# The end of a causal convolution: another split of the last channel block's taps, and a rearranged normalization ahead of the next product

## The chip, the cores and the metric

The kernel runs on one core of one Trainium2 chip. A core has a matrix engine (TensorE, PE in the profile), a vector engine (VectorE, DVE), a scalar engine (ScalarE, ACT) and GpSimd (POOL), each with its own queue of instructions that it works off in order; SP issues the weight loads. Engines wait for each other by semaphores. TensorE reads SBUF and writes PSUM, which has banks of 512 fp32 columns on 128 partitions. The metric is the device time of one execution in microseconds (us); lower is better.

## The reference, cut to what matters

The model is a trunk of two layers for 256 tokens of width 2048, in float32. Layer 0 mixes tokens with a convolution module, layer 1 with latent attention; each is followed by a squared-ReLU MLP. The change touches the convolution module alone:

```python
def conv_module(h, w_pw1, b_pw1, w_dw, b_dw, ln_g, ln_b, w_pw2, b_pw2):
    u = h @ w_pw1 + b_pw1                       # 2048 -> 4096
    a, gate = jnp.split(u, 2, axis=-1)
    u = a * jax.nn.sigmoid(gate)
    u = lax.conv_general_dilated(u, w_dw[:, None, :], window_strides=(1,),
        padding=[(CONV_WIDTH - 1, 0)], ...,     # 31 taps, each channel by itself
        feature_group_count=D_MODEL) + b_dw
    u = jax.nn.silu(layer_norm(u, ln_g, ln_b))  # over the 2048 channels of a token
    return u @ w_pw2 + b_pw2                    # 2048 -> 2048
```

`layer_norm` subtracts the mean over the channels, divides by the root of variance + 1e-5, and applies gain and bias. So the second product can't start before all 2048 channels of the convolution are there.

## The kernel before

**Two products and what stands between.** The channels are worked on in 16 blocks of 128 (`KC`), named c = 0 to 15 here. In the first product `conv_mm` (line 857) leaves a block channel by channel: 128 channels on the partitions, 256 tokens along the row. fp32 numbers are held as a high and a low part (`hi`, `lo`; `sh`, `sl_`), and each product is three matmuls: high by high, low by high, high by low (`mm3`, line 197). For the second product the normalized channels are `sh` and `sl_`, and the weights are `hi` and `lo`.

**Taps.** `glu` (line 880) makes the gated block `ub`, with 30 zeros ahead. The 31 taps of the convolution are a sum of shifted copies of `ub`, each scaled by one weight per channel. DVE does most of them (`dve_tap`, line 957: one instruction for a tap, added into a PSUM tile). ScalarE makes a few scaled copies `tp` (`product`), which POOL adds up (`side_sum`) and DVE joins in (the entry `None` of the list `left`). For the last two blocks TensorE takes taps as matmuls with a diagonal matrix `dg` of weights: 8 for block 14 (`but_one_products`) and `LAST_PE` = 22 for block 15 (`last_products`, line 916). For block 15 that leaves 4 to ScalarE and POOL (`LAST_SIDE`) and 5 to DVE. `dve_taps` (line 982) walks over the blocks that still have taps, oldest first and two by turns, and stops when only `LAST_REST` taps are left; those are done in the next call, behind the next block's `glu`.

**To tokens.** The finished block `ca` is transposed on TensorE into tokens (`to_tokens`, line 1009), two blocks to a PSUM tile `ct`; DVE takes mean and variance of each pair (`bn_stats`, in `ln_stats`, line 1020) and ScalarE copies the pair into `cn`. After the last pair, `bn_aggr` joins the statistics and `rsqrt` (line 216) makes the factor; the root is ScalarE's. ScalarE needs a table for each kind of function; `warm` (line 229) calls one ahead of its use, so that the table is loaded there.

**Normalization.** `ln_norm` (line 1156) applies mean and factor to two blocks of `cn` on DVE; `ln_swish` (line 1164) transposes them back into one PSUM bank (TensorE), applies gain, bias and Silu there (ScalarE, one instruction per block), and makes `sh` (ScalarE) and `sl_` (DVE) from both blocks at once. Three pairs are normalized and two pass `ln_swish` before the second product starts; the third and all later ones are put ahead of the matmuls of an earlier pair.

**Fillers.** `keep_warm` (line 234) issues transposes of the identity on TensorE whose results nobody reads, `N_WARM_LN` = 8, 26 and 14 of them at three places of this stretch.

**What sets the order.** The stretch runs under a manual schedule: every engine has its instructions in the order of the code. Weights come in blocks of 1 MB into three buffers `raw`; a buffer is loaded again when both its halves are split into `hi` (ScalarE) and `lo` (POOL or DVE, `conv_half`, line 844). Behind this stage come the MLP, attention and the second MLP, which this change leaves as they are.

Of the kernel before, what the change touches and what calls it, by code (L numbers as in the profile page):

```python
# [10 lines left out]
F32 = mybir.dt.float32  # L11
# [3 lines left out]
AF = mybir.ActivationFunctionType  # L15
ALU = mybir.AluOpType
# [4 lines left out]
KC = D // P  # L21
T = 2
S = T * P
# [21 lines left out]
PAD_O = 16  # L45
WB = 6
LOOK = WB // 2 - 1
LAST_PE = 22
BUT_ONE_PE = 8
SIDE = 2  # L50
LAST_SIDE = (3, 6, 4)
JOIN = 14
LEAD = 7
REST = (16, 18, 22)
LAST_REST = (20, 9, 0)
FILL_AT = (5, 15)
ORDERS = "STSTSTOSTSTSTSTT", "TSTSTSTOSTSTSTST"
N_S, N_G = 9, 2
# [1 line left out]
MADE = tuple((range(8),) * 3 + (last,) for last in ((0, 2, 1, 3, 4, 5, 6, 7),) * 2)  # L60
LATE_G = ((3, 5, 6, 7), (3, 4, 5, 6, 7))
N_WARM = 14
N_WARM_LN = (8, 26, 14)
EPS = 1e-6
LN_EPS = 1e-5
SCALE = (DN + DR) ** -0.5
# [20 lines left out]
def trunk_kernel(  # L87
# [26 lines left out]
    nc = tc.nc  # L114
# [689 lines left out]
    with ExitStack() as cx:  # L804
# [39 lines left out]
        def conv_half(n, h):  # L844
            if n < NU + KC // 2:
                wjs[n, h] = split_half(raws[n], h, nc.gpsimd if 0 < n + h and (n, h) < (NU + 1, 1) else nc.vector)
# [69 lines left out]
        def last_products(w0, w1):  # L916
            for w in range(w0, w1):
                nc.tensor.matmul(  # L918
                    last_sum[0], dgs[w], ubs[KC - 1][:, w : w + S], start=w == 0, stop=w == LAST_PE - 1
                )  # L920
# [28 lines left out]
        def side_sum(c):  # L949
            ps = sides[c]  # L950
            step = 1
            while step < len(ps):
                for i in range(0, len(ps) - step, 2 * step):
                    nc.gpsimd.tensor_tensor(ps[i], ps[i], ps[i + step], op=ALU.add)
                step *= 2
# [26 lines left out]
        def dve_taps(c, fill):  # L982


            n, last = 0, turns.get("last")
            lead = 0 if c in (0, KC - 1) else LEAD
            while sum(len(v) for v in left.values()) > rest(c):
                ready = [k for k in sorted(left) if left[k] and (k < c or n >= lead)]
                if not ready:
                    break  # L990
                if ready[-1] == KC - 1 and len(left[KC - 1]) == 1 and len(ready) > 1:

                    ready.pop()
                k = next((k for k in ready[:2] if k != last), None)
                if fill and (k is None or n >= FILL_AT[c == KC - 1]):
                    fill.pop(0)()
                if k is None:
                    k = ready[0]
                dve_tap(k)
                if c == KC - 1 and k == KC - 3 and not left[k]:  # L1000

                    to_tokens(k)
                    last_products(LAST_PE // 2, LAST_PE)
                last = turns["last"] = k
                n += 1
            while fill:
                fill.pop(0)()
# [35 lines left out]
        with tc.manual_schedule():  # L1043
# [57 lines left out]
            for c in range(1, KC + 1):  # L1101
                n = UC * c
                conv_load(n + 3)
                if c == KC:
                    but_one_products()
                glu(c - 1)
                fill = ln_stats(c - 4 if c < KC else KC - 3) if c > 3 else []
                fill, copies = fill[:T], fill[T:]
                if c < KC:
                    pss[c] = [acc_tile() for _ in range(2)]  # L1110
                conv_half(n + (c < KC), 0)
                start_sum(c - 1)
                if c < KC:
                    conv_half(n + 1, 1)
                    dve_taps(c - 1, fill)
                    conv_load(n + 4)
                    side_sum(c - 1)
                    conv_mm(c, 0, 8)
                    if c < KC - 1:
                        conv_half(n + 2, 0)  # L1120
                        conv_half(n + 2, 1)
                else:
                    side_sum(c - 1)
                    conv_half(n, 1)
                    conv_half(n + 1, 0)
                    dve_taps(c - 1, fill)
                    conv_load(n + 4)
                for f in copies:
                    f()
                if c < KC:  # L1130
                    conv_mm(c, 8)
                    if c > KC - 4:
                        dgs.extend(diag(KC - 1, w) for w in range(len(dgs), min(len(dgs) + 8, LAST_PE)))
                    if c == KC - 1:
                        but_one.extend(diag(KC - 2, w) for w in range(W - BUT_ONE_PE, W))
                    if c > 2:
                        to_tokens(c - 3)
                    conv_mm(c, 12)
            warm(AF.Sqrt)
            keep_warm(ident, N_WARM_LN[0])  # L1140
            to_tokens(KC - 2)
            to_tokens(KC - 1)
            for f in ln_stats(KC - 1):
                f()
# [19 lines left out]
            def ln_swish(jj):  # L1164
                pt = tr_tile()
                for j in range(2):
                    k = 2 * jj + j
                    for t in range(T):
                        nc.tensor.transpose(
                            pt[:, j * S + t * P : j * S + (t + 1) * P], cn[:, t, k * P : (k + 1) * P], ident  # L1170
                        )
                for j in range(2):
                    k = 2 * jj + j
                    nc.scalar.activation(
                        pt[:, j * S : (j + 1) * S], pt[:, j * S : (j + 1) * S], AF.Silu,
                        bias=ln_b[:, k : k + 1], scale=ln_g[:, k : k + 1],
                    )
                sp = pt.rearrange("p (j n) -> p j n", j=2)
                ks = slice(2 * jj, 2 * jj + 2)
                nc.scalar.activation(sh[:, ks, :], sp, AF.Copy)  # L1180
                nc.vector.tensor_tensor(sl_[:, ks, :], sp, sh[:, ks, :].bitcast(F32), op=ALU.subtract)

            sh_kt = lambda k, t: sh[:, k, t * P : (t + 1) * P]
            sl_kt = lambda k, t: sl_[:, k, t * P : (t + 1) * P]
            NP = KC // 2
# [5 lines left out]
            for m in range(NP):  # L1191
                if m + 3 < NP:
                    ln_norm(m + 3)
                if m + 2 < NP:
                    ln_swish(m + 2)
                for j in range(2):
                    k = 2 * m + j
                    wh, wl = conv_w(NU + m, j)
                    for b in range(2):
                        bs = slice(b * NB, (b + 1) * NB)  # L1200
                        for t in range(T):
                            mm3(ps2[b][t], sh_kt(k, t), sl_kt(k, t), wh[:, bs], wl[:, bs], k == 0, k == KC - 1)
                    if m == 0 and j == 0:
                        conv_half(NU + 1, 1)
                conv_split(NU + m + 2)
                conv_load(NU + m + 5)

                t, i = divmod(m, NNB)
                sl = slice(i * NB, (i + 1) * NB)
                nc.vector.tensor_tensor(xs[:, t, sl], xs[:, t, sl], b2[:, sl], op=ALU.add)  # L1210
# [601 lines left out]
```

## Time and profile before

| What | us |
|---|---|
| time, median of 3 runs (lowest to highest) | 1931.16 (1931.03 to 1931.22) |
| the profiled execution | 1930.93 |
| its span in the trace | 1929.2 |
| TensorE busy in the span | 1904.2 |
| ScalarE's `sg` of block 15 ends | 202.0 |
| last tap rows of block 15 on TensorE start | 205.8 |
| first matmul of the second product starts | 223.9 |

The three last rows are times from the start of the span. In the rows of the trace a name like `ca<-sum,half` is output and inputs, buffer numbers left out; L918 is a line of the kernel; in brackets stands how long the engine was idle before, and who ended that. A row with x22 stands for 22 instructions of one kind in a row: its start is that of the first and its duration reaches to the end of the last. Instructions of an engine overlap, so one that follows starts a little before that end.

### The profile page before, as it was taken

What the parts mean: (1) busy time and instruction counts of PE and PEld (TensorE: products, weight loads), DVE (VectorE), ACT (ScalarE), POOL (GpSimd) and SP (SyncE); (2) the same over time, 40 slices, a digit from 0 to 9 for tenths busy, and PEclk for the clock granted to TensorE, in tenths of its full rate; (3) what the DMA queues carried; (4) which work ended last, traced back from release to release, by engine and by line L of the source; (5) the groups of instructions that cost most, each with busy time, mean ns of one, the idle gap of its engine ahead of it and who ended that gap; (6) DMA issues with size and microseconds to landing.
All of it is one profiled execution on the core that took longest, in us unless ns stands there. A gap on an engine that the chain in (4) does not pass through costs nothing.

```text
span 1929.2 us, 28511 instructions
## 1 busy us (share of the span) xinstructions
PE 1904.2 (99%) x10794; PEld 1669.2 (87%) x10794; DVE 1647.4 (85%) x2367; ACT 1208.2 (63%) x1717; POOL 223.4 (12%) x183
## 2 busy tenths in 40 slices
PE   7999999999999999999999999999999999999998
PEld 7999888888888888888899998888888888888886
DVE  5999865789999999999976665657999999999887
ACT  5556664766666666666566665566666666666654
POOL 5999300000000000000001410000000000000000
PEclk9999999999999999999999999999999999999999
DMA  8676365857666667666646445765667666766663
GB/s 236 187 195 179 129 196 154 234 172 206 203 201 206 197 202 213 200 200 212 205 143 182 118 151 175 205 188 173 199 193 210 208 197 197 217 201 197 212 220 109
DMA packets 407113, 367.62 MB, mean 191 GB/s; under 512 B 15416, under 2 KB 351936, under 8 KB 406720
## 3 DMA queue, kind: packets, MB, share of 16 engines
q1 hardware_dynamic: 405952, 363.63, 63.0%
q10 hardware_dynamic: 1024, 2.17, 0.3%
q8 instruction: 84, 1.38, 0.3%
q14 instruction: 53, 0.43, 0.1%
HBM read 363.68 MB, written 2.10 MB: 190 GB/s over the span
## 4 chain that ended last, share of the span: by engine, by line
PE 88%; DVE 9%; ACT 1%; POOL 1%; DMA 0%; issue 0%; SPq 0%; DVEq 0%; ACTq 0%; POOLq 0%
PE acc L520 24%; PE acc L199 15%; PE acc L200 15%; PE acc L201 15%; PE acc L518 12%; DVE sum L978 7%; PE acc L255 1%; PE sum L918 1%; ACT hi L173 0%; DMA xs<-in_x 0%; PE acc L863 0%; PE acc L864 0%; PE acc L865 0%; PE acc L1580 0%; PE acc L1444 0%
## 5 line engine op out<-in xcount | busy, mean ns | idle before, releaser
L431 DVE TENSOR_TENSOR lo<-raw,hi 128x1024 fp32r<-128x1024 f32 (+1 forms) x512 | 571.7, 1123 | 88.0 <-ACT hi L430 87.6
L430 ACT ACTIVATE hi<-raw 128x1024 fp32r<-128x1024 f32 (+1 forms) x512 | 480.0, 971 | 66.0 <-PE acc L200 65.8
L520 PE MATMUL acc<-xt,hi 128*128 128x512 f32 x2048 | 504.0, 391 | 0.0
L520 PEld LDWEIGHTS acc<-xt,hi 128*128 128x128 f32 x2048 | 374.8, 188 | 72.8 <-ACT hi L430 0.2
L199 PE MATMUL acc<-hi,sh 128*128 128x512 f32 x930 | 362.7, 390 | 0.0
L201 PE MATMUL acc<-lo,sh 128*128 128x512 f32 x930 | 361.9, 389 | 0.0
L200 PE MATMUL acc<-hi,sl 128*128 128x512 f32 x802 | 312.0, 389 | 0.0
L518 PEld LDWEIGHTS acc<-xt,lo 128*128 128x128 f32 x2048 | 257.7, 188 | 10.9
L518 PE MATMUL acc<-xt,lo 128*128 128x256 f32 x2048 | 259.7, 279 | 0.0
L173 ACT ACTIVATE hi<-raw 128x1024 fp32r<-128x1024 f32 (+2 forms) x184 | 180.1, 1006 | 46.2 <-PE acc L200 43.3
L201 PEld LDWEIGHTS acc<-lo,sh 128*128 128x128 f32 x930 | 174.5, 188 | 36.3
L199 PEld LDWEIGHTS acc<-hi,sh 128*128 128x128 f32 x930 | 174.6, 188 | 35.9
L174 DVE TENSOR_TENSOR lo<-raw,hi 128x1024 fp32r<-128x1024 f32 (+2 forms) x118 | 132.9, 1146 | 68.3 <-ACT hi L173 62.3
L430 ACT ACTIVATE hi<-V 128x1024 fp32r<-128x1024 f32 x94 | 99.6, 1060 | 130.7 <-DVE V L726 121.7
L200 PEld LDWEIGHTS acc<-hi,sl 128*128 128x128 f32 x802 | 150.5, 188 | 31.3
L978 DVE SCALAR_TENSOR_TENSOR sum<-ub,w_dw,sum 128x256 f32<-128x256 f32 x392 | 160.0, 512 | 6.4 <-ACT sum L934 5.5
L174 POOL TENSOR_TENSOR lo<-raw,hi 128x1024 fp32r<-128x1024 f32 x66 | 157.7, 2407 | 23.7 <-ACT hi L173 23.1
L430 ACT ACTIVATE hi<-T 128x1024 fp32r<-128x1024 f32 x94 | 99.5, 1058 | 92.5 <-DVE T L714 68.9
L525 ACT ACTIVATE U<-acc 128x512 f32<-128x512 f32 x128 | 75.9, 593 | 108.6 <-PE acc L520 108.6
L863 PE MATMUL acc<-xt,hi 128*128 128x256 f32 x512 | 143.6, 280 | 0.0
L865 PE MATMUL acc<-xt,lo 128*128 128x256 f32 x512 | 142.2, 278 | 0.6 <-POOL lo L174 0.6
L864 PE MATMUL acc<-xt,hi 128*128 128x256 f32 x512 | 142.2, 278 | 0.0
(275 smaller groups left out, 2810.4 us busy)
## 6 DMA issues: line engine op xcount, KB each, us to landing
raw<-in_mlp_w SPq DMA_DIRECT2D x256, 1024.0 KB, 6.2
raw<-in_conv_w_pw SPq DMA_DIRECT2D x64, 512.0 KB, 5.5
raw<-in_conv_w_pw SPq DMA_DIRECT2D x16, 1024.0 KB, 5.0
raw<-in_mla_w_o SPq DMA_DIRECT2D x16, 1024.0 KB, 5.5
raw<-in_mla_w_kv_up SPq DMA_DIRECT2D x8, 1024.0 KB, 5.6
raw<-in_mla_w_in SPq DMA_DIRECT2D x8, 576.0 KB, 3.8
raw<-in_mla_w_in SPq DMA_DIRECT2D x4, 1024.0 KB, 6.0
raw<-in_mla_w_q_up SPq DMA_DIRECT2D x16, 256.0 KB, 3.8
```

What stands on the lines that cost most here:

```text
L173: nc.scalar.activation(hi, raw[:, js, :], AF.Copy)
L174: eng.tensor_tensor(lo, raw[:, js, :], hi.bitcast(F32), op=ALU.subtract)
L199: nc.tensor.matmul(ps, sh, mh, start=start, stop=False)
L200: nc.tensor.matmul(ps, sl, mh, start=False, stop=False)
L201: nc.tensor.matmul(ps, sh, ml, start=False, stop=stop)
L430: nc.scalar.activation(parts[0], src, AF.Copy)
L431: nc.vector.tensor_tensor(parts[1], src, parts[0].bitcast(F32), op=ALU.subtract)
L518: nc.tensor.matmul(ps[0][:, :S], wl[:, j, :], xh(k), start=False, stop=False)
L520: nc.tensor.matmul(ps[0], wh[:, j, :], xhl(k), start=k == 0, stop=k == KC - 1)
L863: nc.tensor.matmul(o, wh[:, bs], xh(k), start=k == 0, stop=False)
L864: nc.tensor.matmul(o, wh[:, bs], xl(k), start=False, stop=False)
L978: nc.vector.scalar_tensor_tensor(out=out, in0=ubs[c][:, w : w + S], scalar=tap(c, w), in1=pcs[c], op0=ALU.mult, op1=ALU.add)
```

## The change

It has six parts, all between the last blocks of the first product and the first of the second.

1. `LAST_PE` goes from 22 to 18 and the last of `LAST_SIDE` from 4 to 6, so that block 15 has 18 taps on TensorE, 6 on ScalarE and POOL, 7 on DVE. ScalarE makes four matrices `dg` less and two copies `tp` more. In SBUF four `dg` buffers of 128 columns go and two `tp` buffers of 256 come.
2. `LAST_REST` for block 14 goes from 9 to 16: seven taps of blocks 13 and 14 move behind block 15's `glu`.
3. The tap matmuls of block 15 come in three pieces, 9, 6 and 3, with the transposes of block 13 and now of block 14 between. The statistics of the pair 12/13 must be issued before block 15's last tap.
4. Block 15's copies `tp` and their additions on POOL come ahead of the splits of the first weights of the second product, no longer between them. `warm(AF.Sqrt)` goes ahead of the last copies into `cn`.
5. The fillers go from 8, 26 and 14 to 4, 20 and 6.
6. The first `ln_swish` makes `sh` and `sl_` of one block at a time. The third comes after the first twelve matmuls of the second product, no longer ahead of them.

```diff
-LAST_PE = 22
+LAST_PE = 18
-LAST_SIDE = (3, 6, 4)
+LAST_SIDE = (3, 6, 6)
-LAST_REST = (20, 9, 0)
+LAST_REST = (20, 16, 0)
-N_WARM_LN = (8, 26, 14)
+N_WARM_LN = (4, 20, 6)
+TOKENS_AT = 3
...
+                if c == KC - 1 and k == c and len(left[c]) == 1:
+                    while fill:
+                        fill.pop(0)()
                 dve_tap(k)
                 if c == KC - 1 and k == KC - 3 and not left[k]:
 
                     to_tokens(k)
-                    last_products(LAST_PE // 2, LAST_PE)
+                    last_products(LAST_PE // 2, LAST_PE - TOKENS_AT)
+                if c == KC - 1 and k == KC - 2 and not left[k]:
+                    to_tokens(k)
+                    last_products(LAST_PE - TOKENS_AT, LAST_PE)
...
-                conv_half(n + (c < KC), 0)
+                if c < KC:
+                    conv_half(n + 1, 0)
                 start_sum(c - 1)
...
                 else:
                     side_sum(c - 1)
+                    conv_half(n, 0)
                     conv_half(n, 1)
                     conv_half(n + 1, 0)
+                    warm(AF.Sqrt)
                     dve_taps(c - 1, fill)
...
-            warm(AF.Sqrt)
             keep_warm(ident, N_WARM_LN[0])
-            to_tokens(KC - 2)
             to_tokens(KC - 1)
...
-                for j in range(2):
-                    k = 2 * jj + j
-                    nc.scalar.activation(
-                        pt[:, j * S : (j + 1) * S], pt[:, j * S : (j + 1) * S], AF.Silu,
-                        bias=ln_b[:, k : k + 1], scale=ln_g[:, k : k + 1],
-                    )
                 sp = pt.rearrange("p (j n) -> p j n", j=2)
-                ks = slice(2 * jj, 2 * jj + 2)
-                nc.scalar.activation(sh[:, ks, :], sp, AF.Copy)
-                nc.vector.tensor_tensor(sl_[:, ks, :], sp, sh[:, ks, :].bitcast(F32), op=ALU.subtract)
-
+                for ks in ((0, 1), (1, 2)) if jj == 0 else ((0, 2),):
+                    for j in range(*ks):
+                        k = 2 * jj + j
+                        nc.scalar.activation(
+                            sp[:, j, :], sp[:, j, :], AF.Silu, bias=ln_b[:, k : k + 1], scale=ln_g[:, k : k + 1]
+                        )
+                    js, ks = slice(*ks), slice(2 * jj + ks[0], 2 * jj + ks[1])
+                    nc.scalar.activation(sh[:, ks, :], sp[:, js, :], AF.Copy)
+                    nc.vector.tensor_tensor(sl_[:, ks, :], sp[:, js, :], sh[:, ks, :].bitcast(F32), op=ALU.subtract)
...
-                if m + 2 < NP:
+                if 0 < m < NP - 2:
                     ln_swish(m + 2)
                 for j in range(2):
+                    if m == 0 and j == 1:
+                        ln_swish(2)
```

On TensorE, from the last taps of block 15 to the first matmuls, before. `ca_3029` holds blocks 14 and 15, `acc_3051` takes their transposes, and `acc_3042<-ident` are fillers:

```order
L918 MATMUL sum_2971<-ub_2961,dg_2913 128x256
L238 MATMUL acc_3042<-ident 128x128 [waits Activation_49]
L238 MATMUL acc_3042<-ident 128x128 x7
L1016 MATMUL acc_3051<-ident,ca_3029 128x128 [waits DVE_49]
L1016 MATMUL acc_3051<-ident,ca_3029 128x128
```

And in the changed kernel, where `ca_3024` holds blocks 14 and 15:

```order
L919 MATMUL sum_2952<-ub_2946,dg_2729 128x256
L1023 MATMUL acc_3026<-ident,ca_3024 128x128 [waits DVE_49,Activation_49]
L1023 MATMUL acc_3026<-ident,ca_3024 128x128
L919 MATMUL sum_2952<-ub_2946,dg_2731 128x256
L919 MATMUL sum_2952<-ub_2946,dg_2896 128x256
L919 MATMUL sum_2952<-ub_2946,dg_2898 128x256
L239 MATMUL acc_3041<-ident 128x128 x4
L1023 MATMUL acc_3026<-ident,ca_3024 128x128 [waits DVE_49]
```

Block 14's transposes have moved from behind the fillers to between the tap matmuls, three of which now stand behind their wait for DVE.

On DVE, the same stretch before, from block 14's last tap (`half_3027`; `tr_2923` is the pair 12/13, `acc_2970` block 15's sum):

```order
L972 SCALAR_TENSOR_TENSOR half_3027<-ub_2761,w_dw,sum_2774 128x256 [waits DVE_49]
L975 TENSOR_TENSOR ca_3029<-acc_2952,half_3027 128x256 [waits DVE_49,PE_49]
L961 TENSOR_TENSOR acc_2970<-acc_2970,tp_2983 128x256 [waits Pool_49]
L1026 BN_STATS stats<-tr_2923 128x6 [waits PE_49]
L972 SCALAR_TENSOR_TENSOR half_3033<-ub_2961,w_dw,acc_2970 128x256 [waits DVE_49]
L975 TENSOR_TENSOR ca_3029<-sum_2971,half_3033 128x256 [waits DVE_49,PE_49]
L1026 BN_STATS stats<-tr_2923 128x6
```

And in the changed kernel, from the first statistics of 12/13 (`tr_2908`; block 15's sum is `acc_2951`):

```order
L1033 BN_STATS stats<-tr_2908 128x6 [waits PE_49]
L962 TENSOR_TENSOR sum_2774<-sum_2774,tp_2776 128x256 [waits DVE_49,Pool_49]
L1033 BN_STATS stats<-tr_2908 128x6
L979 SCALAR_TENSOR_TENSOR acc_2951<-ub_2946,w_dw,acc_2951 128x256 [waits DVE_49]
L979 SCALAR_TENSOR_TENSOR sum_2774<-ub_2761,w_dw,sum_2774 128x256 [waits DVE_49]
L979 SCALAR_TENSOR_TENSOR acc_2951<-ub_2946,w_dw,acc_2951 128x256 [waits DVE_49]
L973 SCALAR_TENSOR_TENSOR half_3022<-ub_2761,w_dw,sum_2774 128x256 [waits DVE_49]
L976 TENSOR_TENSOR ca_3024<-acc_2937,half_3022 128x256 [waits DVE_49]
L979 SCALAR_TENSOR_TENSOR acc_2951<-ub_2946,w_dw,acc_2951 128x256
L979 SCALAR_TENSOR_TENSOR acc_2951<-ub_2946,w_dw,acc_2951 128x256 [waits DVE_49]
L962 TENSOR_TENSOR acc_2951<-acc_2951,tp_2962 128x256 [waits DVE_49,Pool_49]
L973 SCALAR_TENSOR_TENSOR half_3035<-ub_2946,w_dw,acc_2951 128x256 [waits DVE_49]
```

The statistics of 12/13, with their wait for TensorE, now stand ahead of block 14's last taps, and between the `ca` of block 14 and that of block 15 there are four instructions that each need the one before.

On ScalarE, from the last copies into `cn` to the first Silus, before:

```order
L1028 ACTIVATE cn<-tr_2923 128x2x256 [waits DVE_49,PE_49,Activation_49]
L232 ACT_TABLE_LOAD
L232 ACTIVATE warm_3040<-ident 128x1
L1028 ACTIVATE cn<-acc_3051 128x2x256 [waits DVE_49,PE_49,Activation_49]
L222 ACTIVATE t_3091<-v_3089 128x2 [waits DVE_49]
```

And in the changed kernel, up to the second half of the first `ln_swish`:

```order
L233 ACT_TABLE_LOAD
L233 ACTIVATE warm_2991<-ident 128x1
L1035 ACTIVATE cn<-tr_2908 128x2x256 [waits DVE_49,PE_49,Activation_49]
L1035 ACTIVATE cn<-acc_3026 128x2x256 [waits DVE_49,PE_49,Activation_49]
L223 ACTIVATE t_3077<-v_3075 128x2 [waits DVE_49]
L233 ACT_TABLE_LOAD
L233 ACTIVATE warm_3084<-ident 128x1 [waits Activation_49]
L1184 ACTIVATE acc_3102<-acc_3102,vecs_cv 128x256 [waits PE_49]
L1188 ACTIVATE sh<-acc_3102 128x256 [waits Activation_49]
L1184 ACTIVATE acc_3102<-acc_3102,vecs_cv 128x256 [waits DVE_49]
L1188 ACTIVATE sh<-acc_3102 128x256 [waits Activation_49]
```

The load of the root's table has moved ahead of both copies, and the second Silu of the first `ln_swish` now waits for DVE, which reads the first half of the same bank.

## The prediction

> **What bounds the kernel now.** I read the page first (span, chain), then who TensorE waits for, and then the order of time on PE, DVE and ACT from 196 to 225 us, where the convolution ends and its second product begins.
>
> ```profile
> span 1929.2 us, 28511 instructions
> ...
> PE 88%; DVE 9%; ACT 1%; POOL 1%; DMA 0%; issue 0%; SPq 0%; DVEq 0%; ACTq 0%; POOLq 0%
> ...
> PE sum L918 <- DVE ub L888: 0.9, 1, 0.9
> ...
> PE acc L1169 <- DVE cn L1159: 0.7, 1, 0.7
> ```
>
> The span is made of TensorE work. Two of TensorE's waits lie at the place of the change: 0.9 us for the last channel's `ub`, 0.7 us for the first normalized columns. The rest of what can be won there is hidden behind filler, transposes of `ident` (L238), which count as busy. So the measure is how long it takes from the end of the first product to the first real matmuls of the second. In order of time on PE (start, duration, how many; a fp32 product of a tap shows as two rows):
>
> ```profile
> 201.31 3.61 PE L926 MATMUL acc<-ub,cn 128*128 128x256 f32 x16
> 205.78 5.02 PE L918 MATMUL sum<-ub,dg 128*128 128x256 f32 x22 [0.86 <-DVE ub L888]
> 210.63 0.38 PE L1016 MATMUL tr<-ident,ca 128*128 128x128 f32 x2
> 210.85 4.92 PE L918 MATMUL sum<-ub,dg 128*128 128x256 f32 x22
> 215.61 1.03 PE L238 MATMUL acc<-ident 128*128 128x128 f32 x8
> 216.48 0.60 PE L1016 MATMUL acc<-ident,ca 128*128 128x128 f32 x4
> ...
> 220.65 1.52 PE L1169 MATMUL acc<-ident,cn 128*128 128x128 f32 x8 [0.74 <-DVE cn L1159]
> ...
> 223.54 0.60 PE L1169 MATMUL acc<-ident,cn 128*128 128x128 f32 x4
> 223.89 0.48 PE L199 MATMUL acc<-hi,sh 128*128 128x512 f32 x1
> 224.21 0.39 PE L200 MATMUL acc<-hi,sl__123 128*128 128x512 f32 x1
> 224.44 0.40 PE L201 MATMUL acc<-lo,sh 128*128 128x512 f32 x1
> ```
>
> On DVE and then ACT:
>
> ```profile
> 196.95 8.38 DVE L978 SCALAR_TENSOR_TENSOR sum<-ub,w_dw,sum 128x256 f32<-128x256 f32 x21
> 205.21 0.51 DVE L888 SCALAR_TENSOR_TENSOR ub<-acc,vecs_cv,sg 128x256 f32<-128x256 f32 x1
> ...
> 206.75 0.54 DVE L978 SCALAR_TENSOR_TENSOR ca<-ub,w_dw,sum 128x256 f32<-128x256 f32 x1
> ...
> 208.76 0.49 DVE L961 TENSOR_TENSOR sum<-sum,tp 128x256 f32<-128x256 f32 x1
> ...
> 210.27 0.55 DVE L972 SCALAR_TENSOR_TENSOR half<-ub,w_dw,sum 128x256 f32<-128x256 f32 x1
> 210.91 0.42 DVE L975 TENSOR_TENSOR ca<-acc,half 128x256 f32<-128x256 f32 x1
> ...
> 211.59 0.42 DVE L1026 BATCH_NORM_STATS2 stats<-tr 128x6 f32<-128x256 f32 x1
> 211.93 0.46 DVE L972 SCALAR_TENSOR_TENSOR half<-ub,w_dw,acc 128x256 f32<-128x256 f32 x1
> 215.81 0.42 DVE L975 TENSOR_TENSOR ca<-sum,half 128x256 f32<-128x256 f32 x1 [3.42 <-PE sum L918]
> ...
> 217.12 0.76 DVE L1026 BATCH_NORM_STATS2 stats<-acc 128x6 f32<-128x256 f32 x2 [0.54 <-PE acc L1016]
> ...
> 218.41 0.17 DVE L221 TENSOR_SCALAR v<-mv 128x2 f32<-128x2 f32 x1
> ...
> 220.19 2.03 DVE L1159 TENSOR_SCALAR cn<-cn,mv,y 128x256 f32<-128x256 f32 x6
> 223.33 0.69 DVE L1181 TENSOR_TENSOR sl__123<-acc,sh 128x512 fp32r<-128x512 f32 x1 [1.12 <-ACT sh L1180]
> ```
>
> ```profile
> 201.57 0.47 ACT L885 ACTIVATE sg<-acc,vecs_cv 128x256 f32<-128x256 f32 x1
> ...
> 205.76 1.71 ACT L898 ACTIVATE tp<-ub,w_dw 128x256 f32<-128x256 f32 x4 [2.77 <-DVE ub L888]
> ...
> 217.29 1.28 ACT L232 ACT_TABLE_LOAD   x1
> ...
> 218.69 0.58 ACT L1028 ACTIVATE cn<-acc 128x512 f32<-128x512 f32 x1
> 219.17 0.19 ACT L222 ACTIVATE t<-v 128x2 f32<-128x2 f32 x1
> ...
> 221.56 1.11 ACT L1174 ACTIVATE acc<-acc,vecs_cv 128x256 f32<-128x256 f32 x2 [0.68 <-PE acc L1169]
> 222.70 0.60 ACT L1180 ACTIVATE sh<-acc 128x512 fp32r<-128x512 f32 x1
> ```
>
> To be seen: DVE stands still for 3.42 us until TensorE has done all 22 taps of channel 15; the square root at 219.17 comes behind a table load and a copy though `v` is ready at 218.58; the first matmul stands behind fourteen fillers and four transposes.
>
> **The change, step by step.** Times of the changed kernel are worked out on the clock of these rows.
>
> *Last `ub` ahead of seven taps.* A tap of DVE costs (205.21 - 196.95)/21 = 0.393 us. With seven taps fewer ahead, `ub` starts at 196.95 + 14 x 0.393 = 202.46; its other input `sg` ends at 202.04. So it is there at 202.97, before TensorE needs it: L926's sixteen rows let the next start at about 204.77. The wait of 0.86 us goes; the taps only change places.
>
> *Eighteen taps on TensorE instead of 22, in three pieces.* A row costs (210.63 - 205.78)/22 = 0.22 us, in the second piece (215.61 - 210.85)/22 = 0.216. Eighteen rows from 204.77 end at 208.74; the transposes of channel 13 (0.38) at 209.12. `ca` of channel 13 ends, as before, at 207.29. Twelve more rows end at 208.96 + 2.60 = 211.56.
>
> *DVE takes two of the four taps, ScalarE two.* Up to 208.76 DVE has the same number of instructions, and the first `bn_stats` of the pair 12/13 now stands there and waits for the transposes: 0.4 us, and all of DVE's remaining taps queue behind it. From 209.16: statistics, join, statistics at 0.34 each (211.93 - 211.59), three taps (1.18), the `half` step until its `ca` 0.64 (210.27 to 210.91): channel 14's `ca` starts at 212.00, ends at 212.42. TensorE has waited for it since 211.56, 0.9 us, with the last six tap rows behind it: they start at 212.46 + 0.22 and the last ends near 214.14. DVE meanwhile goes on at 212.34 with two taps, join, `half`, each needing the one before. A chain of dependent taps is in this row:
>
> ```profile
> 35.00 7.32 DVE L978 SCALAR_TENSOR_TENSOR sum<-ub,w_dw,sum 128x256 f32<-128x256 f32 x14 [4.37 <-ACT sum L934]
> ...
> 206.75 2.33 POOL L954 TENSOR_TENSOR tp<-tp,tp 128x256 f32<-128x256 f32 x3 [1.33 <-ACT tp L898]
> 209.04 4.67 POOL L174 TENSOR_TENSOR lo<-raw,hi 128x1024 fp32r<-128x1024 f32 x2
> ```
>
> It gives 0.53 a step; the 0.64 above is the other bound. Four steps are 2.1 to 2.5 us; I take 2.25, since taps are nearer to the first and the joins to the second. Channel 15's `ca` starts at 214.59 instead of 215.81; the end is now set by DVE, 0.4 us behind TensorE.
>
> *Six side products, and POOL's order.* ScalarE makes six products (0.43 each) from 203.0 to 205.6, and three splits follow. POOL makes five additions of 0.78 from about 203.9, to 207.9, then three `lo` splits of 2.34: to 214.9, where they ended at 213.7. The join needs POOL at 213, the first matmul at 221: both costs are zero, with 5 and 6 us of cover. The weight buffer behind them comes free about 1.2 us later, near 212.6, so the load that SP issues into it starts later too; its data, the fourth block, is split only behind the first block of matmuls, after 226, so this also costs nothing.
>
> *Channel 14 transposed early, four fillers instead of eight.* Before, channel 15's `ca` was ready at 216.23 and its transposes stood behind eight fillers and channel 14's (216.48 to 217.08). Now fillers are over by 214.5, and two transposes start at 215.05, 0.04 after `ca` ends at 215.01; they take 0.38. The last statistics start at 215.47 instead of 217.12: 1.65 us earlier.
>
> *The Sqrt table early.* Its load now lies at about 208.5, where ScalarE has nothing to do until the statistics of 12/13. After the last statistics `v` needs 1.46 us (217.12 to 218.58) and the copy of `cn` ends its issue at 0.76 + 0.04 + 0.48 = 1.28, so the root starts 1.50 after them, not 2.05: at 216.97 instead of 219.17, 2.20 earlier. The 1.02 us to the first normalization and the 1.37 us from there to the first Silu stay: 217.99 and 219.36. The Silu table (another 1.28) is in by 218.7.
>
> A table load here delays the next instruction by 1.28 us and no more: the copy at 218.69 follows the load's end (218.57) by 0.12. The Trainium skill's page "ScalarE: Activation LUTs", section "What ACT_TABLE_LOAD costs", gives the same 1.28 us but adds a drain of 1.38 us to each switch; by that the first Silu would start near 220.0 and the sum would be 0.7 us smaller. The trace does not show that drain, and I go by the trace.
>
> *Half a block first.* One Silu (0.56), `sh` of 256 columns, `sl` of 256 columns, then the matmul, instead of two Silus, 512 and 512. Neither half form is in the trace: `sh` lies between 0.43 (a `tp`) and 0.60 (222.70), `sl` between 0.42 (L975) and 0.69 (223.33). The low rows are of the same size and the high ones twice as wide, so I take the low ends. Silu to 219.94, `sh` to 220.37, `sl` 220.41 to 220.83; the first matmul at 220.41 (six fillers end about then too) and the second at 220.88 instead of 224.21: 3.33 earlier. High ends cost 0.44 more. The second half now waits for the first `sl`, and is done near 222.3; the block that needs it starts at about 223.85, since twelve matmuls of 0.23 hide it. That is its cover of 1.5 us.
>
> *Transposes of block 2 moved behind the first twelve matmuls.* They cost what they cost ahead of them, 0.35 (223.54 to 223.89) and 0.09 in the slower first matmul: 0.44 us that come back.
>
> **Sum.** -1.65 (last statistics), -0.55 (root), -1.13 (the rest of 3.33: fillers and half block), +0.44 (transposes): -2.89 us. Behind this point TensorE has no waits for what the change touches, so the gain should last. The profiled execution took 1930.93 us (span 1929.2 and 1.7 around it), 0.2 below the median of 1931.16. So the median comes out at about 1928.3. With TensorE instead of DVE ending last it is 0.4 better, with both high ends 0.7 worse: 1927.8 to 1929.0 for this case.
>
> **Rivals.** *DVE gets no earlier.* Two more taps and a wait for transposes sit on DVE. If the chain from 209.16 to channel 15's `ca` takes 6.6 us instead of 5.4, that `ca` stays at 215.81, only the later steps win, and the time is 1929.5. For it speaks the serial chain; against it, that every step of it has a price above.
>
> *TensorE's clock drops.* Fillers fall from 48 to 30, and gaps of 0.9 (at 211.6), 0.6 (214.5) and 0.9 us (217.5) stand in ten microseconds. What slow means here the kernel's start shows:
>
> ```profile
> 12.24 3.19 PE L238 MATMUL acc<-ident,xs 128*128 128x128 f32 x14
> ...
> 220.00:224.00 4.00, 3.35 (x27) 2.96 (x27) 2.85 (x8) 3.21 (x7) 0.00 (x0) 1.00 0.00 0
> ```
>
> Fourteen transposes took 3.19 us, 0.22 each, against 0.11 in the row at 215.61: half rate, for 3.2 us, a loss of 1.6. The same at the first matmuls gives 1929.9. Two such stretches lose 3.2 and end at 1931.5, slower than before; 5.8 us at half rate is where it turns, and 13.5 us would make it slower by 0.2%, 3.9 us, which is about what a measurement of this kernel can tell from no change. Against it: from 220 to 224 the granted clock is 1.00 with 0.65 us idle, and matmuls after 8 us of transposes alone run at 0.23. The Trainium skill's "TensorE: Matmul & The Clock Gate" would have it otherwise: "Part 1: The HAM clock gate" halves the clock after an idle window of about 3.4 us, and "Part 4: PE-mode transpose" says that transposes do not count as busy in the same way. By that rule the stretch was cold before as well, and the trace does not agree; it would leave 1929.9 only if the new gaps decide.
>
> *More than 0.2% faster.* It needs another 1.0 us: TensorE ending last (0.4) and the statistics chain shorter by 0.6. No row gives the 0.6.
>
> **How the numbers follow.** Forecast 0.71; DVE no earlier 0.09; one cold stretch 0.07; slower than before through the clock 0.07, of which 0.04 beyond 0.2%; over 0.2% faster 0.06. The range of 1927.4 to 1930.0 takes in the first three. Faster 0.06, same 0.90, slower 0.04.
>
> **What would show it.** Right: no wait of L919 for `ub`; about 0.4 us of DVE waiting for transposes ahead of `bn_stats` on `tr`; TensorE waiting 0.9 us for channel 14; channel 15's `ca` near 214.6 with little idle time before it; the root near 217; the second matmul near 220.9 and the block after it without a wait; nothing new later. Wrong: 128x512 matmuls of 0.4 us issued 0.46 apart behind 220 (clock), a wait for the second `sl`, or a transfer that TensorE waits for.

## The result, and the profile after

The changed kernel takes 1928.07 us (median of 20 runs, 1927.48 to 1929.39), the kernel before 1931.13 us on the same chip (20 runs, 1930.69 to 1932.07). The ratio is 0.9984, with a 95% interval from 0.9978 to 0.9990: 3.06 us less, 0.16%, within the 0.2% that the prediction called no change, and 0.2 us from its 1928.3.

The profiled execution has a span of 1926.2 us, 3.0 less than before. First TensorE in order of time, from the last tap rows of channel 15 to the matmuls of the second product:

```profile
204.83 4.05 PE L919 MATMUL sum<-ub,dg 128*128 128x256 f32 x18
208.71 0.38 PE L1023 MATMUL tr<-ident,ca 128*128 128x128 f32 x2
208.93 2.76 PE L919 MATMUL sum<-ub,dg 128*128 128x256 f32 x12
212.39 0.41 PE L1023 MATMUL acc<-ident,ca 128*128 128x128 f32 x2 [0.70 <-DVE ca L976]
...
214.80 0.44 PE L1023 MATMUL acc<-ident,ca 128*128 128x128 f32 x2 [0.27 <-DVE ca L976]
215.07 2.35 PE L239 MATMUL acc<-ident 128*128 128x128 f32 x20
218.27 1.52 PE L1177 MATMUL acc<-ident,cn 128*128 128x128 f32 x8 [0.85 <-DVE cn L1167]
219.62 0.82 PE L239 MATMUL acc<-ident 128*128 128x128 f32 x6
220.20 0.49 PE L200 MATMUL acc<-hi,sh 128*128 128x512 f32 x1
220.64 0.50 PE L201 MATMUL acc<-hi,sl__123 128*128 128x512 f32 x1
```

The wait for `ub` is gone. In its place stands the wait of 0.70 us for channel 14's `ca`. DVE and ScalarE over the same stretch:

```profile
209.13 0.43 DVE L1033 BATCH_NORM_STATS2 stats<-tr 128x6 f32<-128x256 f32 x1
...
211.82 0.42 DVE L976 TENSOR_TENSOR ca<-acc,half 128x256 f32<-128x256 f32 x1
212.16 1.00 DVE L979 SCALAR_TENSOR_TENSOR acc<-ub,w_dw,acc 128x256 f32<-128x256 f32 x2
213.27 0.43 DVE L962 TENSOR_TENSOR acc<-acc,tp 128x256 f32<-128x256 f32 x1
213.74 0.48 DVE L973 SCALAR_TENSOR_TENSOR half<-ub,w_dw,acc 128x256 f32<-128x256 f32 x1
214.32 0.42 DVE L976 TENSOR_TENSOR ca<-sum,half 128x256 f32<-128x256 f32 x1
215.28 0.76 DVE L1033 BATCH_NORM_STATS2 stats<-acc 128x6 f32<-128x256 f32 x2 [0.53 <-PE acc L1023]
```

```profile
208.45 1.28 ACT L233 ACT_TABLE_LOAD   x1
...
210.35 0.60 ACT L1035 ACTIVATE cn<-tr 128x512 f32<-128x512 f32 x1 [0.40 <-DVE stats L1033]
216.15 0.60 ACT L1035 ACTIVATE cn<-acc 128x512 f32<-128x512 f32 x1 [5.21 <-DVE stats L1033]
216.78 0.20 ACT L223 ACTIVATE t<-v 128x2 f32<-128x2 f32 x1
...
219.18 0.54 ACT L1184 ACTIVATE acc<-acc,vecs_cv 128x256 f32<-128x256 f32 x1 [0.68 <-PE acc L1177]
219.75 0.38 ACT L1188 ACTIVATE sh<-acc 128x256 fp32r<-128x256 f32 x1
220.62 0.54 ACT L1184 ACTIVATE acc<-acc,vecs_cv 128x256 f32<-128x256 f32 x1 [0.49 <-DVE sl__123 L1189]
```

Channel 15's `ca` (214.32) now follows its `half` step without idle time: DVE ends the chain, not TensorE. The last statistics are 1.84 us earlier than before, the root 2.39. The gain can be read at the first point where both kernels do the same work with the same work behind it, the transposes of the fourth pair, in the order of time of PE before

```profile
229.47 0.60 PE L1169 MATMUL acc<-ident,cn 128*128 128x128 f32 x4
```

and after:

```profile
226.48 0.60 PE L1177 MATMUL acc<-ident,cn 128*128 128x128 f32 x4
```

That is 2.99 us, the whole difference of the spans. Behind it nothing was given back.

### The profile page after: what moved, and what is told of

Read it like the earlier page. It is cut to its first block, busy times and chain, and to the rows that moved or that the text cites. A ratio compares the mean times of both kernels' runs of the same rounds, so it can differ in the third digit from the quotient of the medians.

```text
span 1926.2 us, 28463 instructions
## 1 busy us (share of the span) xinstructions
PE 1900.7 (99%) x10768; PEld 1665.0 (86%) x10768; DVE 1648.4 (86%) x2370; ACT 1206.5 (63%) x1716; POOL 224.6 (12%) x185
## 3 DMA queue, kind: packets, MB, share of 16 engines
q8 instruction: 84, 1.38, 0.3%
## 4 chain that ended last, share of the span: by engine, by line
PE 88%; DVE 8%; ACT 2%; POOL 1%; issue 1%; DMA 1%; DVEq 0%; ACTq 0%; POOLq 0%
PE acc L521 24%; PE acc L201 15%; PE acc L200 15%; PE acc L202 15%; PE acc L519 12%; DVE sum L979 6%; POOL lo L175 1%; PE acc L256 1%; ACT hi L174 1%; PE acc L866 0%; PE acc L865 0%; PE acc L864 0%; PE acc L1589 0%; DMA xs<-in_x 0%; PE acc L1453 0%
```

## The experiments

Theory: the gain is the sum of steps that lie one behind the other, and each step can be undone for its own price. The rivals: TensorE's clock, DVE as the new bound, and that a step's price sits elsewhere than where the prediction put it. Each further version was run 9 to 11 times beside 31 to 33 runs of the kernel before on the same chip, so the medians (us) are compared by the distance to it; the changed kernel has -3.06 us by that measure.

| Kernel | before | this | distance |
|---|---|---|---|
| changed kernel | 1931.13 | 1928.07 | -3.06 |
| old fillers | 1930.87 | 1928.52 | -2.35 |
| no fillers | 1930.87 | 1929.36 | -1.51 |
| Sqrt call at its old place | 1930.87 | 1927.92 | -2.95 |
| first pair whole | 1930.87 | 1928.82 | -2.05 |
| 22 taps on TensorE | 1930.97 | 1928.62 | -2.35 |
| before, only `ub` early | 1930.97 | 1929.25 | -1.72 |
| third pair ahead again | 1930.97 | 1927.64 | -3.33 |
| statistics of 12/13 later | 1930.97 | 1927.39 | -3.58 |
| no middle fillers | 1930.88 | 1929.02 | -1.86 |
| two banks | 1930.88 | 1927.63 | -3.25 |
| late statistics, third pair ahead | 1930.88 | 1926.79 | -4.09 |
| all of these | 1930.88 | 1926.30 | -4.58 |

Most of these differ from each other by less than 0.1%, about what the 95% interval of each ratio to the kernel before leaves open to either side, so times alone do not tell neighbours apart. They are told apart by their traces, where a step is placed to some 0.05 us; the start of this stretch wanders by 0.2 us between executions, in two of them by about 1.3, so distances within one are read.

### Fillers

```diff
-N_WARM_LN = (4, 20, 6)
+N_WARM_LN = (8, 26, 14)
```

> The changed kernel with the old numbers of fillers, 8, 26 and 14. Theory (fillers are only queue in front of real work): the first eight end at 213.94 + 8 x 0.11 = 214.8, when channel 15's transposes can start anyway, the 26 end at 217.9, ahead of the 218.3 at which the normalized columns come, and only the last fourteen are in the way: they end near 221.2, so the second matmul starts near 221.5 instead of 220.64 and the time is 0.8 us above the changed kernel, 1928.9. Rival (fillers keep TensorE's clock up): no change or a little faster than the changed kernel, 1928.1 or less.

Measured: 0.71 us of the gain are gone. TensorE goes from the last fillers straight to the matmuls, its order of time:

```profile
219.64 1.51 PE L1177 MATMUL acc<-ident,cn 128*128 128x128 f32 x8 [0.19 <-DVE cn L1167]
220.99 1.69 PE L239 MATMUL acc<-ident 128*128 128x128 f32 x14
222.44 0.48 PE L200 MATMUL acc<-hi,sh 128*128 128x512 f32 x1
222.76 0.40 PE L201 MATMUL acc<-hi,sl__123 128*128 128x512 f32 x1
```

From the first transposes to the first matmul are 2.80 us, against 1.93 in the changed kernel; to the second matmul, for which the changed kernel waits for `sl_`, 3.12 against 2.37. The last fourteen were in the way, the first two groups were not. This execution reaches the stretch some 1.4 us late. More fillers bring no speed: matmuls start 0.23 us apart in both.

```diff
-            keep_warm(ident, N_WARM_LN[0])
...
-            keep_warm(ident, N_WARM_LN[1])
...
-            keep_warm(ident, N_WARM_LN[2])
```

> The changed kernel without the three groups of fillers between the two products. Theory (fillers are only queue): the first matmul is held by the first sh, which ends at 220.13, so nothing or 0.1 us is won: 1928.0. Rival (TensorE's clock falls when nothing is issued): TensorE then has gaps of 1.5, 3 and 1 us; matmuls after them are issued 0.46 us apart instead of 0.23 for some 3 us, and the time is 1929.7, or more if it lasts longer.

Measured: 1.55 us slower than the changed kernel in the median; the profiled execution, at 1930.20 us, is 0.84 above that median. My theory fell and the rival held. In the windows of this run the third column from the right is the granted clock of TensorE:

```profile
214.00:218.00 4.00, 0.51 (x3) 0.20 (x2) 2.92 (x12) 1.83 (x3) 0.75 (x1) 1.00 0.66 254
218.00:220.00 2.00, 1.75 (x8) 1.54 (x8) 1.80 (x6) 0.95 (x3) 0.00 (x0) 0.54 0.00 0
...
222.00:224.00 2.00, 2.00 (x6) 1.62 (x5) 0.80 (x2) 1.94 (x4) 0.00 (x0) 0.50 0.00 0
224.00:226.00 2.00, 2.00 (x10) 1.57 (x10) 2.00 (x4) 0.48 (x1) 0.00 (x0) 0.75 0.00 0
```

and in its order of time the gap and the matmuls:

```profile
218.25 2.08 PE L1175 MATMUL acc<-ident,cn 128*128 128x128 f32 x8 [3.03 <-DVE cn L1165]
...
222.42 0.63 PE L201 MATMUL acc<-hi,sl__123 128*128 128x512 f32 x1
222.85 0.63 PE L202 MATMUL acc<-lo,sh 128*128 128x512 f32 x1
```

At the end of a gap of 3.03 us the clock goes to 0.5, from about 218.2 to 225.0, and matmuls start 0.43 us apart instead of 0.23. So fillers do carry the clock, and the question was which of them.

```diff
-            keep_warm(ident, N_WARM_LN[1])
```

> The changed kernel without its twenty middle fillers; four before and six behind stay. TensorE then has one gap of 3.0 us, 215.2 to 218.3. Theory (the kernel without any filler showed half clock from 218 on, and this gap is the cause): the same half clock from 218 to about 225, matmuls 0.43 us apart, the six fillers behind now cost 0.22 each on top: 1929.5 to 1930.3. Rival (it took all gaps together, or the missing fillers right ahead of the matmuls): full clock and 1928.0.

Measured: 1.20 us slower than the changed kernel, less than expected. The clock falls at the same place, and comes back earlier:

```profile
218.00:220.00 2.00, 1.93 (x9) 1.79 (x10) 1.63 (x6) 0.92 (x4) 0.00 (x0) 0.50 0.00 0
220.00:222.00 2.00, 2.00 (x11) 1.87 (x10) 0.66 (x2) 1.48 (x4) 0.00 (x0) 0.72 0.00 0
222.00:224.00 2.00, 2.00 (x11) 1.58 (x10) 0.80 (x3) 1.94 (x4) 0.00 (x0) 1.00 0.00 0
```

```profile
219.94 1.41 PE L239 MATMUL acc<-ident 128*128 128x128 f32 x6
...
221.41 0.39 PE L201 MATMUL acc<-hi,sl__123 128*128 128x512 f32 x1
```

The gap of 3.0 us alone takes the clock down; the gaps of 0.70 and 0.27 us ahead of it, which stay, do not. By the windows it is half from about 217.7 to 221.1, 3.4 us, and at the first matmul it is full again, with nothing but transposes run since: 0.39 us for the second matmul, where the run without fillers has 0.63. The middle twenty are the ones that pay.

### The root and the statistics

```diff
-                    warm(AF.Sqrt)
                     dve_taps(c - 1, fill)
...
+            warm(AF.Sqrt)
             keep_warm(ident, N_WARM_LN[0])
```

> The changed kernel with the call that loads the Sqrt table at its old place, behind the copy of the pair 12/13. Theory: that copy itself has moved, to 210.35, because its statistics now come early; the load then stands at about 210.9 to 212.2, four microseconds ahead of the root, and the time stays: 1928.1. So the 0.55 us that the prediction booked under the early table would come from the early statistics. Rival (the prediction's wording, the place of the call is what counts): the root starts 0.55 us later and the time is 1928.6.

Measured: no change (-2.95 against -3.06). ScalarE loads the table behind the copy of 12/13, and the root starts where it did:

```profile
210.92 1.28 ACT L233 ACT_TABLE_LOAD   x1
...
216.75 0.20 ACT L223 ACTIVATE t<-v 128x2 f32<-128x2 f32 x1
```

The place of the call is worth nothing once the copy ahead of it is early. The other way round, the kernel before with one number changed:

```diff
-LAST_REST = (20, 9, 0)
+LAST_REST = (20, 16, 0)
```

> The kernel before with one number changed: 16 taps instead of 9 are left behind the last ub. Theory: TensorE's 22 taps start at 204.8 instead of 205.8 and end 1.0 us earlier, DVE has been waiting for them, and everything behind follows: channel 15's ca at 214.8, time 1930.1. Rival (DVE gets no earlier, because the taps only change places): ca stays at 215.8 and the time at 1931.1.

Measured: 1.72 us faster than before, more than the 1.0 of my theory. DVE, ScalarE:

```profile
209.77 0.43 DVE L1026 BATCH_NORM_STATS2 stats<-tr 128x6 f32<-128x256 f32 x1 [1.03 <-PE tr L1016]
...
210.45 0.42 DVE L1026 BATCH_NORM_STATS2 stats<-tr 128x6 f32<-128x256 f32 x1
...
214.53 0.42 DVE L975 TENSOR_TENSOR ca<-sum,half 128x256 f32<-128x256 f32 x1 [0.79 <-PE sum L918]
215.84 0.76 DVE L1026 BATCH_NORM_STATS2 stats<-acc 128x6 f32<-128x256 f32 x2 [0.89 <-PE acc L1016]
```

```profile
210.98 0.60 ACT L1028 ACTIVATE cn<-tr 128x512 f32<-128x512 f32 x1 [4.54 <-DVE stats L1026]
211.58 1.28 ACT L232 ACT_TABLE_LOAD   x1
...
217.34 0.20 ACT L222 ACTIVATE t<-v 128x2 f32<-128x2 f32 x1
```

The last statistics are 1.28 us earlier, as expected within 0.3. The root comes 1.50 us behind them, not 2.05, with the table call where it always was. The list of taps is longer, so the fixed place of the statistics in it (`FILL_AT`, behind 15 steps) now lies ahead of channel 15's last tap; the copy follows them, and the table load follows the copy. One number alone gives 1.7 us, where all parts give 3.06.

### Division of the taps

```diff
-LAST_PE = 18
+LAST_PE = 22
-LAST_SIDE = (3, 6, 6)
+LAST_SIDE = (3, 6, 4)
```

> The changed kernel with the old division of the last channel's taps: 22 on TensorE, 4 on ScalarE and POOL, 5 on DVE; the order of all else stays. Theory: eight more tap rows of 0.216 us on TensorE, four of them ahead of the transposes of channel 13. The first statistics of 12/13 then start at 210.0 instead of 209.13, and the last tap row ends at 214.9, so channel 15's ca starts at 214.97 instead of 214.32, now set by TensorE: 0.65 us above the changed kernel, 1928.7. Rival (the new division is what made the last statistics earlier): channel 15's ca falls back to 215.8 and the time is 1929.6 or more.

Measured: 0.71 us slower than the changed kernel, as expected, and the end is TensorE's again, on DVE:

```profile
214.97 0.42 DVE L976 TENSOR_TENSOR ca<-sum,half 128x256 f32<-128x256 f32 x1 [1.04 <-PE sum L919]
```

Four taps off TensorE bring 0.65 us at this point, not the 1.7 that their eight rows take: the rest of what they could bring is DVE's chain.

### The first pair and the third

```diff
-                for ks in ((0, 1), (1, 2)) if jj == 0 else ((0, 2),):
+                for ks in ((0, 2),):
```

> The changed kernel with the first pair's Silu, sh and sl for both blocks at once, as before. Theory: two Silus 219.18 to 220.28, sh of 512 columns to 220.91, sl of 512 to 221.64; the second matmul starts at 221.7 instead of 220.64, and the time is 1.05 us above the changed kernel: 1929.1. Rival (the second half pays back what the first gains, because its Silu waits for DVE on the same bank): no change, 1928.1.

Measured: 1.01 us slower than the changed kernel, as expected. TensorE waits for `sh` and `sl_` of both blocks:

```profile
220.87 0.50 PE L200 MATMUL acc<-hi,sh 128*128 128x512 f32 x1 [0.53 <-ACT sh L1188]
221.60 0.50 PE L201 MATMUL acc<-hi,sl__123 128*128 128x512 f32 x1 [0.23 <-DVE sl__123 L1189]
```

The second half's wait for DVE takes nothing back. That was tried by itself too, with a PSUM bank for each block of the first pair:

```diff
-                pt = tr_tile()
+                pts = [tr_tile() for _ in range(2 if jj == 0 else 1)]
+                sps = [pt.rearrange("p (j n) -> p j n", j=2) for pt in pts]
...
-                            pt[:, j * S + t * P : j * S + (t + 1) * P], cn[:, t, k * P : (k + 1) * P], ident
+                            sps[-j][:, j, t * P : (t + 1) * P], cn[:, t, k * P : (k + 1) * P], ident
...
                 for ks in ((0, 1), (1, 2)) if jj == 0 else ((0, 2),):
+                    sp = sps[-ks[0]]
```

> The changed kernel with the first pair's two blocks in a PSUM bank each, so that the first Silu waits for two transposes instead of four and the second no longer for DVE. Theory: the second sl is done 0.6 us earlier, which nobody waits for; the first Silu starts 0.22 earlier, but the six fillers end only at 220.27, so the second matmul starts at about 220.52 instead of 220.64: 0.1 us faster. Rival (the second Silu's wait for DVE is on the path): 0.4 us or more faster.

Measured: -3.25, 0.2 us faster than the changed kernel. The first Silu starts 0.25 earlier (it waits for two transposes), the second matmul 0.16 earlier, at 220.48. The second `sl_` is done 0.85 us earlier and nobody waits for it: the second block of matmuls starts 0.24 earlier, no more than the third matmul of the first block does (220.73 against 220.98).

```diff
-                if 0 < m < NP - 2:
+                if m + 2 < NP:
                     ln_swish(m + 2)
...
-                    if m == 0 and j == 1:
-                        ln_swish(2)
```

> The changed kernel with the third pair's transposes ahead of the first matmuls again, behind the six fillers. Theory: fillers end at 220.27, four transposes take 0.36, the second matmul starts at 220.95 instead of 220.64, but the 0.44 us between the first and the second block of twelve matmuls are gone: 0.1 to 0.25 us faster than the changed kernel, 1927.9. Rival (moving them was a gain): 0.3 us or more slower, 1928.4.

Measured: -3.33, 0.27 us faster than the changed kernel. Its first and third matmul:

```profile
220.47 0.48 PE L200 MATMUL acc<-hi,sh 128*128 128x512 f32 x1
...
221.02 0.39 PE L202 MATMUL acc<-lo,sh 128*128 128x512 f32 x1
```

They start 0.55 us apart, in the changed kernel 0.78. From channel 15's `ca` to the fourth pair's transposes are 11.85 us (214.16 to 226.01) instead of 12.16, so moving the third pair's transposes behind the first matmuls was a small loss.

### Three more versions that beat the changed kernel

```diff
-FILL_AT = (5, 15)
+FILL_AT = (5, 21)
```

> The changed kernel with the two statistics of 12/13 six places further back on DVE, between the last dependent taps of channel 15. Theory: DVE no longer waits for the transposes of channel 13 with channel 14's taps queued behind; channel 14's ca starts at 210.9 instead of 211.82, TensorE no longer waits 0.7 us for it, and the statistics fill gaps between dependent taps; channel 15's ca starts at 213.75 instead of 214.32: 1927.5. Rival (the end is set by the dependent chain behind channel 14 alone, and two more instructions in it cost their 0.34 each): ca of 15 at 214.2 or later, 1928.0.

Measured: -3.58, 0.52 us faster than the changed kernel. DVE no longer waits for channel 13's transposes ahead of channel 14's taps:

```profile
210.94 0.42 DVE L976 TENSOR_TENSOR ca<-acc,half 128x256 f32<-128x256 f32 x1
...
213.76 0.42 DVE L976 TENSOR_TENSOR ca<-sum,half 128x256 f32<-128x256 f32 x1
```

Between dependent steps the statistics cost about half: from one `ca` to the other are 2.82 us with two of them between, 2.50 without, so 0.16 each, where the next instruction starts 0.35 behind one of them in the changed kernel (209.13, 209.48).

With this, the third pair ahead of the matmuls and the six last fillers left out for it (`N_WARM_LN` 4, 20, 0):

> The changed kernel with the statistics of 12/13 six places further back, and the third pair's transposes ahead of the matmuls in place of the six last fillers. Theory: the two gains add, since they lie one behind the other: 0.56 us (channel 15's ca at 213.76) and 0.44 us (the transposes take the fillers' place): 1.0 us faster than the changed kernel, 1927.0. Rival (without the last fillers the clock falls): 1928.0 or more.

Measured: -4.09, 1.03 us faster than the changed kernel. The two gains add, and leaving out the last six fillers brings some 0.2 more: from channel 15's `ca` to the fourth pair's transposes are 11.69 us (214.56 to 226.25), 0.16 less than with the third pair ahead alone. The clock stays at 1.00 without these six.

And with the two banks, and one tap more on ScalarE and POOL, for which the late statistics move one place forward (the buffers for `tp` stay at 15):

```diff
-LAST_SIDE = (3, 6, 6)
+LAST_SIDE = (3, 6, 7)
-FILL_AT = (5, 15)
+FILL_AT = (5, 20)
```

> As the one before, with the two banks, and with one more tap of channel 15 moved from DVE to ScalarE and POOL (18, 7 and 6). Theory: one dependent step less on DVE between the ca of channels 14 and 15, so that of 15 at 213.4, 0.37 earlier; two banks 0.2: 1926.4. Rival (TensorE's last tap rows, which end near 213.3, or POOL's six additions take over): 1926.9.

Measured: 1926.30 us against 1930.88, ratio 0.9976 (0.9966 to 0.9986), 1.5 us faster than the changed kernel. Its `ca` and its second matmul:

```profile
213.24 0.42 DVE L976 TENSOR_TENSOR ca<-sum,half 128x256 f32<-128x256 f32 x1
```

```profile
219.42 0.42 PE L201 MATMUL acc<-hi,sl__123 128*128 128x512 f32 x1
```

## Why the prediction was right, and where it was not

**The sum held:** -2.89 us worked out, -3.06 measured, -2.99 in the traces. Part of that closeness is luck: the second matmul came 3.57 us earlier, not 3.33, and from there 0.58 were given back, not 0.44. The transposes cost the 0.44 as priced; most of the rest is the third matmul, 0.34 behind the second instead of 0.23. The single points came out at most 0.27 us early: channel 14's `ca` at 211.82 (212.00 in the prediction), channel 15's at 214.32 (214.59), the last statistics at 215.28 (215.47), the root at 216.78 (216.97), the first Silu at 219.18 (219.36), the second matmul at 220.64 (220.88), the next block at 223.63 (223.85).

**The early `ub`** was there at 203.0 and its wait gone, as said.

**The three pieces.** TensorE's wait for channel 14 was 0.70 us where 0.9 was worked out, since DVE's chain was 0.2 shorter ahead of it: channel 14's `half` until its `ca` took 0.51 (211.31 to 211.82), not 0.64. DVE's own wait for channel 13's transposes was 0.14 us (208.99 to 209.13), not 0.4. The four dependent steps took 2.16 us (212.16 to 214.32), at the low end of 2.1 to 2.5: the two taps 1.11 together, the join 0.47, the `half` until its `ca` 0.58. That DVE, and not TensorE, then ends the chain is shown from both sides: with four taps back on TensorE the end is TensorE's, with one tap less on DVE there are 2.43 us from one `ca` to the other (210.81 to 213.24) instead of 2.82.

**The Sqrt table: right size, but not the cause that was named.** "The Sqrt table early" booked 0.55 us to the table call's new place. The root did start 1.50 us behind the statistics. But with the call at its old place it did as well, and in the kernel before with `LAST_REST` alone too. What suffices for the 0.55 is the early place of the statistics of 12/13 on DVE: the copy waits for them, and the table load stood behind the copy. Whether the early call would have brought it with the statistics at their old place, no run shows. The prediction saw that these statistics had moved, and priced only the wait that this put on DVE.

**The half block** gave 1.0 us, shown by undoing it with the new fillers in place. The `sh` of 256 columns took 0.38, less than the 0.43 taken, and the `sl_` 0.42, as taken. But half block and fillers do not add, against the theory that each step has its own price. From the first transposes to the second matmul the kernel before took 3.56 us (220.65 to 224.21), the changed one 2.37: both together gained 1.19, of which 0.35 are the third pair's transposes, no longer there. Undone singly, the fillers cost 0.75 and the half block 1.06 at this point, since the later of fillers and `sl_` sets the matmul. The prediction had them in one term, 1.13.

**The transposes behind the matmuls** were priced at 0.44 us, which the trace confirms, but the prediction did not ask whether leaving them ahead was cheaper: it was, by 0.27 us, because TensorE stands waiting for the first `sl_` anyway (0.78 us from the first matmul to the third, 0.55 with the transposes ahead).

**The rivals.** *DVE gets no earlier* is out. *The clock drops* did not happen in the changed kernel: it is 1.00 in every window from 205 to 230. But the rival's mechanism is real, and its price of 1.6 us for one stretch was near: 1.55 and 1.20 us in the medians of the two versions without the middle fillers. That was in part luck: the row from which it was taken (fourteen transposes from 12.24) shows half the rate, but the granted clock reads 1.00 there (12 to 16 us), so the row does not show that the clock was its cause. The prediction gave the rival its chance without asking which fillers keep it away: it is the twenty in the middle, and the thirty are not alike. *More than 0.2% faster* stayed out with the changed kernel; of the 0.6 us for which it found no row, the late statistics are 0.52, and with the other steps 1926.30 us is 0.24% below the kernel before.

**The rules of the Trainium skill.** A load of a table still delays what follows by its 1.28 us alone (208.45, and the warm-up behind it at 209.74 by the end of the load): no drain of 1.38 us shows, so the trace differs from the Trainium skill's "ScalarE: Activation LUTs", "What ACT_TABLE_LOAD costs". Of the Trainium skill's "TensorE: Matmul & The Clock Gate", "Part 1: The HAM clock gate" (half the clock after an idle window of about 3.4 us, and a window of work to get it back) agrees roughly with the two runs with a gap of 3.0 us, which is a little shorter already and enough; half clock then lasted 6.8 us without any fillers and 3.4 without the middle ones, about two and one of these windows. In the run without fillers TensorE was at work for most of the first 3.4 us too, and yet the clock stayed down; why, is open. What the same page of the Trainium skill says in "Part 4: PE-mode transpose", that transposes do not count as busy in the same way, does not agree: transposes alone held the clock at 1.00 for 6 us in the changed kernel, and they alone ran ahead of its return, after 3.4 us, in the run without the middle fillers. The profile lists them as MATMUL; whether they run in the mode that the page means, it does not say.

## What to carry to other kernels

Where one engine hands on to another in short steps, write down for each step which engine comes last, and move the work that nobody waits for yet out of the queue of that engine: the single number that puts `ub` ahead of seven taps brought more than half of the gain. An instruction with a free place, such as the statistics here, belongs between dependent steps, not ahead of them; steps that end at the same wait, such as fillers and half block here, are priced together; and what is booked to an early table load should be tried with the load at its old place. Fillers are to be judged one group at a time: one group kept the clock, another stood in the way.

## What the runs showed of the hardware

Not expected: a gap of 3.0 us on TensorE, behind a stretch that was busy, halves its clock (0.50), and matmuls of 512 columns then start 0.43 us apart instead of 0.23. Gaps of 0.70, 0.27 and 0.85 us within seven microseconds in the changed kernel do not. The half clock lasted 6.8 us in the profile without fillers (218.2 to 225.0) and 3.4 in that without the middle ones (217.7 to 221.1), and cost 2.2 and 0.7 us at the fourth pair's transposes (228.68 and 227.14 against 226.48). That the six fillers made the difference is not shown, for executions of one kernel differ as much: without fillers four of eleven took 1928.70 to 1928.85 us at a mean granted clock of 0.998, the other seven 1929.12 to 1930.82 at 0.996 or 0.997; without the middle ones nine took 1928.60 to 1929.36 at 0.998, two 1929.81 and 1931.04 at 0.997. So the medians' 1.55 and 1.20 us may well be mixtures of short and long stretches.
